# Block 1's first MLP matrix in pairs of tiles, by seven half-width products instead of eight

## The chip, the cores and the metric

The kernel runs on one core of one Trainium2 chip. The metric is the device time of one execution in microseconds; the median of three runs of the kernel before is 1555.03 us (1554.95 to 1555.81). The names used for the engines are those of the profile: PE (TensorE, matmuls), PEld (its weight loads), DVE (VectorE), ACT (ScalarE), POOL (GpSimd) and SP (SyncE, which here only issues DMAs).

## The reference

The whole program is a model of two blocks on 512 tokens of width 1024, in float32. Block 1 is a hybrid mixer (spatial gating and a gated delta rule), cross-attention to a memory of 256 tokens, and a squared-relu MLP; block 2 is a convolution and windowed attention with rotary positions, and a gated MLP. The change concerns block 1's MLP:

```
def squared_relu_mlp(h, w1, w2):
    return jnp.square(jax.nn.relu(h @ w1)) @ w2
...
    x = x + squared_relu_mlp(rmsnorm(x, norm_ffn[l]), ffn_w1[l], ffn_w2[l])
```

Here w1 is 1024 x 4096 and w2 is 4096 x 1024.

## The kernel before

Activations lie feature-major in SBUF: a tile has 128 features on the partitions and 512 tokens in its columns, so x is eight such tiles. A product with a weight matrix is made in output tiles of 128 features; each takes, for every k tile of 128 input features, three matmuls of 512 columns. Float32 precision comes from splitting both operands into a high part (rounded to fp32r) and a low part (the remainder), and from adding high x high, high x low and low x high in PSUM: `mm3`, lines 252 to 254.

The weights arrive in one fixed list (`weight_order`), eight 128x128 tiles to a unit of [128 x 1024]. `prefetch` loads a unit by DMA into one of four buffers `raw` (SP, in written order), ScalarE casts it to `whi` (L217) and VectorE subtracts to get `wlo` (L219); `PF` says that loads run three units ahead and splits one. `defer(n, fn)` puts other work off by n weight tiles of the list. The Tile framework orders the instructions of each engine other than SP; each engine then executes its own list in that order, and waits on semaphores for the other engines.

Block 1's MLP makes its 4096 hidden features, 32 tiles, in four groups of eight. `hidden(n)` makes one tile of h @ w1: 24 matmuls, relu on ScalarE (L1129), a square on VectorE (L1130) and the split into parts (L320 on ScalarE, L321 on VectorE). After eight hidden tiles (and one of the next group, so that TensorE has something to do) come eight tiles of the second matrix, each with k over the group's eight hidden tiles; VectorE multiplies the result by `rb2` (L1145), the row of 1/rms^2 over all tokens, and GpSimd adds it to x (L1147). The norm's row can be multiplied in at the end because the hidden features scale with it; it comes from the sum of squares `acc` of x, which `wide_later` (L402) spreads over all partitions with two matmuls against a matrix of ones (L407 for acc's high part, L408 for its low part), followed by L410 and a reciprocal (L411). It is asked for three weight tiles into the MLP.

Just ahead of the MLP stands the last product of the attention (`xa_wo`): its eight output tiles are added to x (L1090) and split right away, as operands of w1. Behind it the code writes block 2's rotary tables (L1099 to L1120): position times frequency, reduced by multiples of 2 pi, then ScalarE's sine twice (`sinT`, `cosT`). They are small work for VectorE and ScalarE that is carried out beside the first hidden tiles.

Buffers: activations share 74 slots of [128 x 512] (names beginning with t, also `acc`); `whi` and `wlo` have three buffers each.

Of the kernel before, what the change touches and what calls it, by code (L numbers as in the profile page):

```python
# [32 lines left out]
# parts, before a rotation (its halves are swapped by DMA), before block 2's first norm  # L33
# [12 lines left out]
# ---------------------------------------------------------------- weights  # L46
def weight_order():
    """(matrix, k tile, n tile) of the 128x128 weight tiles, as consumed."""
    seq = []

# [26 lines left out]
    for g in range(4):  # L77
        cols("ffn_w1", range(8 * g + (1 if g else 0), 8 * g + 8), r8)
        if g < 3:
            cols("ffn_w1", [8 * g + 8], r8)  # L80
        cols("ffn_w2", r8, range(8 * g, 8 * g + 8))
    # block 2: cb 0-7, cc 8-15, cx 16-23, q 24-27, k 28, v 29, g_conv 30-37, g_attn 38-45
# [14 lines left out]
    return seq  # L97
# [4 lines left out]
# per-partition columns: (name, columns)  # L102
# [13 lines left out]
# constants of the shapes: identity, ones, upper triangle, decay masks, inversion masks  # L116
# [4 lines left out]
def build(tc, A, out, stage=99):  # L121
    nc = tc.nc
    ctx = ExitStack()
    with ctx:
        # loads are issued in the order in which they are written
        ctx.enter_context(tc.manual_schedule(engines={mybir.EngineType.SP}))
        _build(ctx, tc, nc, A, out, stage)


def _build(ctx, tc, nc, A, out, stage):  # L130
# [33 lines left out]
    # ------------------------------------------------------------ loads  # L164
# [24 lines left out]
    # ------------------------------------------------------------ weights  # L189
    order = weight_order()  # L190
# [5 lines left out]
    def prefetch(u, ahead, split_ahead):  # L196
        """half-units of weights from u on: loads, then high and low parts"""
# [7 lines left out]
        for v in range(u, min(u + split_ahead, nu - 1) + 1):  # L205
            if v not in wsp:
# [16 lines left out]

    late = []
# [10 lines left out]
    def nxt(name, k, n, c=1):  # L235
# [4 lines left out]
        if i % 8 == 0:  # L240
            wraw.pop(u - 1, None)
            wsp.pop(u - 1, None)
            prefetch(u, *PF)
        hi, lo = wsp[u]
# [5 lines left out]
    def mm3(ps, ahi, alo, bhi, blo, start, stop):  # L250
        """ps += a.T @ b, a and b given as high and low parts."""
# [4 lines left out]
    def ling(name, n, ks, mv, ps, start=True, stop=True, off=0):  # L256
        """one output tile; a generator, so that other work can go in between"""
# [14 lines left out]
    # ------------------------------------------------------------ interleaving  # L272
    bg = deque()

    def fill(us):
        """the next pieces of background work"""
        t = 0.0
        while bg and t < us:
# [5 lines left out]
            if d is None:      # waits for the chains  # L284
                break
# [82 lines left out]
    def colsum(acc, nt):  # L368
        """token-major column sums over the partitions: [128, nt] in PSUM"""
# [5 lines left out]
    def row_bc(c, nt, dst=None):  # L375
        """[128, nt] columns spread over all partitions as a row of nt*128"""
# [16 lines left out]
    def norm_later(acc, eps, r, at):  # L393
        """r = rstd columns of the squares' sum acc, emitted a few weight tiles later"""
# [7 lines left out]
    def wide_later(acc, eps, rbt, at, square):  # L402
        """rbt = the row of rstd (or its square) over all partitions, a few weight tiles later"""
# [43 lines left out]
    def conv4(ps, j, lst):  # L447
        """causal convolution of 4 taps and silu of projection tile j"""
# [36 lines left out]
    # w_ab: 8 columns of logits, feature-major  # L485
# [13 lines left out]
    def decay():  # L499
        """beta and the decays from their logits"""  # L500
# [19 lines left out]
        # softplus(a) = max(a, 0) + log1p(exp(-|a|)), log1p(e) = 2 atanh(e / (2 + e))  # L520
# [31 lines left out]
        # running and total decay of each chunk of 128  # L552
# [10 lines left out]
    # ------------------------------------------------ gated delta rule, chunks of 128  # L563
# [44 lines left out]
        # k stays as it is: its norms' squares scale the rows of N, which leaves N's inverse  # L608
        # similar, and the values' rows then carry one norm
# [7 lines left out]
        # the blocks of 16 on the diagonal of N, one to a partition  # L617
# [10 lines left out]
    def inv16():  # L628
        """inverses of I - N in all blocks of 16, transposed"""
# [11 lines left out]
    def qprep():  # L641
        """the part that needs q"""
# [24 lines left out]
    def prep2(c):  # L667
# [6 lines left out]
        # U is the inverse of the diagonal blocks of I - N transposed, doubled in size at each step  # L674
# [19 lines left out]
        # the last two doublings have one block (of 32, then 64) above each diagonal  # L694
# [71 lines left out]
    def out_g(c, ET, vn, state):  # L766
        """chunk c of the delta rule's output: normed, feature-major and gated"""
# [16 lines left out]
        # rmsnorm over dv; q's scale comes in here  # L784
# [66 lines left out]
    # ------------------------------------------------ spatial gating; the delta rule's gate  # L851
# [56 lines left out]
    def mix_g():  # L908
        # lower triangle of the mixing weights, transposed [s, g, t]
# [87 lines left out]
    # w_out  # L997
# [12 lines left out]
    # ============================================================ block 1: cross-attention  # L1010
# [76 lines left out]
    xs2 = []  # L1087
    for n in range(8):
        ps = pss[n] if n < 4 else lin("xa_wo", n, range(8), os_)
        V.tensor_add(x[n], x[n], ps)  # L1090
        xs2.append(split(x[n], col("norm_ffn", n)))
        square_acc(acc, x[n], n == 0, eng=V if n == 7 else G)
    if stage == 2:
# [28 lines left out]
    # ============================================================ block 1: squared relu MLP  # L1122
# [3 lines left out]
    def hidden(n):  # L1126
        ps = lin("ffn_w1", n, range(8), xs)
        r = tmp()
        S.activation(r, ps, AF.Relu)  # L1129
        V.tensor_mul(r, r, r)  # L1130
        return split(r)

    hs = []
# [5 lines left out]
    for g in range(4):  # L1139
# [481 lines left out]
```

## Time and profile before

| | before |
|---|---|
| median of 3 runs | 1555.03 us |
| range of the runs | 1554.95 to 1555.81 us |
| span of the profiled execution, which is the only time shown of it | 1555.8 us |
| PE busy | 1534.2 us, 99% |
| PEld busy | 1263.5 us, 81% |
| DVE busy | 926.7 us, 60% |
| ACT busy | 624.7 us, 40% |
| POOL busy | 135.7 us, 9% |
| the MLP of block 1 | 415.10 to 770.70 us |

Busy time is a share of the whole span, over stages of different kinds; the MLP of block 1 is a little under a quarter of it. A matmul's row begins when it is issued and its end is modelled, so rows of consecutive matmuls overlap, and the step from one start to the next is what a matmul costs in a row of them. A row that ends in square brackets tells how long the engine stood idle ahead of it and what ended this. [...]

### The profile page before, as it was taken

Reading aid. Unit: us, or ns where it says so; the run is one execution under the profiler, and the core shown is the slowest. Engines: PE = TensorE matmul, PEld = TensorE weight load, DVE = VectorE, ACT = ScalarE, POOL = GpSimd, SP = SyncE. Lnnn points to the kernel's source line nnn. Section 1 sums busy time; section 2 is a strip of 40 time slices with the busy share of each in tenths; the row PEclk is TensorE's granted clock in tenths of the full one; section 3 lists DMA queues with packets and bytes.
Section 4 is the critical chain, followed back from the end, with each engine's and each line's share of the span. In section 5 each row is a group of like instructions: output and inputs, shape, how many; then the busy total and the mean of one; then the engine's idle time right before and its main releaser. Section 6 shows DMA issues by size and latency. Waiting matters only on the chain.

```text
span 1555.8 us, 18997 instructions
## 1 busy us (share of the span) xinstructions
PE 1534.2 (99%) x7400; PEld 1263.5 (81%) x7400; DVE 926.7 (60%) x1501; ACT 624.7 (40%) x1043; POOL 135.7 (9%) x162
## 2 busy tenths in 40 slices
PE   8999999999999999999999999999999999999996
PEld 6888798888888888888888888888888888888886
DVE  6887575554665454454588777335546555555557
ACT  6665555443442322324544444333334331332243
POOL 0002120200201011010500000000020002001101
PEclk9999999999999999999999999999999999999998
DMA  7133135221322332222134222223322222322321
GB/s 248 29 105 122 58 125 200 95 68 55 102 95 95 95 95 95 95 95 95 54 99 138 86 77 82 82 95 95 95 95 94 94 86 96 101 94 87 102 74 55
DMA packets 51499, 149.80 MB, mean 96 GB/s; under 512 B 9552, under 2 KB 14032, under 8 KB 51408
## 3 DMA queue, kind: packets, MB, share of 16 engines
q1 hardware_dynamic: 51264, 148.32, 29.5%
q8 instruction: 58, 0.95, 0.2%
q10 hardware_dynamic: 144, 0.26, 0.1%
q14 instruction: 33, 0.27, 0.1%
HBM read 143.97 MB, written 3.28 MB: 95 GB/s over the span
## 4 chain that ended last, share of the span: by engine, by line
PE 97%; DVE 2%; ACT 0%; DMA 0%; issue 0%; SPq 0%; DVEq 0%; ACTq 0%
PE mm L252 30%; PE mm L254 30%; PE mm L253 30%; PE sm L254 1%; PE sm L252 1%; PE sm L253 1%; DVE wlo L219 0%; DMA raw<-wts 0%; PE sm L372 0%; PE sm L710 0%; PE sm L1327 0%; PE sm L1329 0%; PE sm L1328 0%; PE sm L504 0%; PE sm L701 0%; PE sm L580 0%
## 5 line engine op out<-in xcount | busy, mean ns | idle before, releaser
L252 PE MATMUL mm<-t,whi 128*128 128x512 f32 (+1 forms) x1944 | 761.7, 392 | 7.9 <-ACT whi L213 7.4
L253 PE MATMUL mm<-t,whi 128*128 128x512 f32 (+1 forms) x1944 | 758.3, 390 | 0.0
L254 PE MATMUL mm<-t,wlo 128*128 128x512 f32 (+1 forms) x1944 | 758.0, 390 | 0.1
L217 ACT CAST whi<-raw 128x1024 fp32r<-128x1024 f32 x254 | 266.4, 1051 | 594.1 <-PE mm L253 409.8
L219 DVE TENSOR_TENSOR wlo<-raw,whi 128x1024 fp32r<-128x1024 f32 x254 | 354.7, 1396 | 151.8 <-ACT whi L217 147.7
L252 PEld LDWEIGHTS mm<-t,whi 128*128 128x128 f32 x1944 | 365.9, 188 | 87.2 <-ACT whi L213 7.4
L254 PEld LDWEIGHTS mm<-t,wlo 128*128 128x128 f32 x1944 | 365.5, 188 | 83.1 <-DVE wlo L219 1.0
L253 PEld LDWEIGHTS mm<-t,whi 128*128 128x128 f32 x1944 | 365.8, 188 | 79.0
L366 POOL TENSOR_TENSOR acc<-acc,tmp 128x512 f32<-128x512 f32 (+1 forms) x37 | 52.9, 1437 | 499.6 <-ACT tmp L362 243.6
L1145 DVE TENSOR_TENSOR tmp<-mm,acc 128x512 f32<-128x512 f32 x32 | 22.1, 692 | 72.6 <-PE mm L254 72.6
L320 ACT CAST t<-tmp 128x512 fp32r<-128x512 f32 (+1 forms) x70 | 41.6, 596 | 51.0 <-DVE tmp L1130 44.8
L1188 DVE TENSOR_TENSOR tmp<-mm,acc 128x512 f32<-128x512 f32 x46 | 31.7, 689 | 49.0 <-PE mm L254 48.3
L321 DVE TENSOR_TENSOR t<-tmp,t 128x512 fp32r<-128x512 f32 (+1 forms) x70 | 46.0, 657 | 23.3 <-ACT t L320 23.1
L1147 POOL TENSOR_TENSOR res<-res,tmp 128x512 f32<-128x512 f32 x24 | 31.0, 1291 | 245.8 <-DVE tmp L1145 237.2
L1428 DVE TENSOR_TENSOR zp<-mm,acc 128x512 f32<-128x512 f32 x22 | 15.2, 691 | 54.7 <-PE mm L254 54.7
L1444 POOL TENSOR_TENSOR res<-res,tmp 128x512 f32<-128x512 f32 x16 | 20.7, 1293 | 261.5 <-DVE tmp L1443 261.5
L1431 DVE TENSOR_TENSOR tmp<-tmp,mm 128x512 f32<-128x512 f32 x22 | 15.1, 686 | 42.7 <-PE mm L254 41.9
L1443 DVE TENSOR_TENSOR tmp<-mm,acc 128x512 f32<-128x512 f32 x16 | 11.1, 691 | 39.6 <-PE mm L254 39.6
L1339 DVE SCALAR_TENSOR_TENSOR tmp<-zp,colt,tmp 128x512 f32<-128x512 f32 x44 | 32.9, 749 | 2.5 <-ACT tmp L1337 1.7
L1430 ACT ACTIVATE tmp<-tmp,colt 128x512 f32<-128x512 f32 x22 | 15.9, 724 | 41.8 <-DVE tmp L1339 41.8
L456 DVE SCALAR_TENSOR_TENSOR tmp<-zp,colt,tmp 128x512 f32<-128x512 f32 x36 | 26.9, 748 | 5.8 <-ACT tmp L452 5.4
L362 ACT ACTIVATE tmp<-res 128x512 f32<-128x512 f32 (+1 forms) x47 | 26.0, 566 | 10.4 <-DVE res L1505 10.4
(349 smaller groups left out, 1356.3 us busy)
## 6 DMA issues: line engine op xcount, KB each, us to landing
raw<-wts SPq DMA_DIRECT2D x259, 512.0 KB, 3.5
res<-xT SPq DMA_DIRECT2D x16, 256.0 KB, 5.3
yT<-t SPq DMA_DIRECT2D x6, 256.0 KB, 2.3
tmp<-tmp SPq DMA_DIRECT2D x20, 64.0 KB, 2.0
gm<-gm SPq DMA_DIRECT2D x4, 256.0 KB, 4.3
dn<-ch SPq DMA_DIRECT2D x4, 256.0 KB, 2.3
tmp<-memT SPq DMA_DIRECT2D x4, 256.0 KB, 2.6
cst<-const SPq DMA_DIRECT2D x1, 576.0 KB, 6.7
```

The costliest lines, as they stand in the source:

```text
L217: S.copy(hi, r)
L219: defer(LO, lambda r=r, hi=hi, lo=lo: V.tensor_sub(lo, r, hi.bitcast(F32)))
L252: PE.matmul(ps, lhsT=ahi, rhs=bhi, start=start, stop=False)
L253: PE.matmul(ps, lhsT=ahi, rhs=blo, start=False, stop=False)
L254: PE.matmul(ps, lhsT=alo, rhs=bhi, start=False, stop=stop)
L320: S.copy(hi, src)
L321: V.tensor_sub(lo, src, hi.bitcast(F32))
L366: eng.tensor_add(acc[:, :w], acc[:, :w], dst[:, :w])
L456: V.scalar_tensor_tensor(out=c, in0=zp[:, 1 + i:1 + i + T], scalar=col("dn_conv", 4 * j + i), in1=c, op0=ALU.mult, op1=ALU.add)
L1147: G.tensor_add(x[n], x[n], t)
L1188: V.tensor_mul(t, ps, rb)
L1339: V.scalar_tensor_tensor(out=c, in0=zp[:, 2 + i:2 + i + T], scalar=col(wname, 3 * j + i), in1=c, op0=ALU.mult, op1=ALU.add)
```

## The change

The first matrix is multiplied in pairs of output tiles. A pair's weights are a matrix of 256 hidden features by 1024 inputs; the k tiles are taken in four pairs (even and odd), so that weights form 2x2 blocks of 128x128, and the tokens are halved into two lots of 256 columns. A 2x2 product of blocks normally needs eight block products; Strassen's algorithm in Winograd's form needs seven, of sums of blocks. So a pair has seven products of four k steps with three matmuls of 256 columns each (84) where two hidden tiles had 48 matmuls of 512 columns.

The sums are made elsewhere. `seven_steps` makes, per pair, the left sums from the raw weights: `s75` (1024 columns wide), `s64` (two halves of 512), and the parts of a (1024), s75, s64 and b (512): three wide casts and one of 512 on ScalarE, three wide subtractions and one of 512 on VectorE. `rights` makes the sums of token halves once, while `xa_wo` finishes. `pairg` runs the products in the order of `SEVEN`, and four VectorE operations from PSUM combine them into `q`, after a ScalarE copy `c0` of the first product. Relu, square and high parts are now ScalarE's, the low parts VectorE's, both put off by `QD`. `ffn_order` sets the order of the pairs and tiles: four pairs, then for each group a pair, four tiles of w2, a pair, four tiles of w2, and two pairs. `whi` and `wlo` get five buffers, of which a pair takes three; activations have 67 slots.

```diff
-NSLOT = 74
-NRAW, NWS = 4, 3
+NSLOT = 67
+NRAW, NWS = 4, 5
+NSR, NQ = 2, 2
+SPREAD = [6, 2]
+QD = [2, 4]
...
+def ffn_order():
+    for i in range(4):
+        yield 1, i, 0
+    for g in range(4):
+        for n in range(8):
+            if g < 3 and n % 4 == 0:
+                yield 1, 4 * g + 4 + n // 4, g + 1
+            yield 2, n, g
+        if g < 3:
+            yield 1, 4 * g + 6, g + 1
+            yield 1, 4 * g + 7, g + 1
...
+    def sevens(u, later):
+        if u not in sevp:
+            load_raw(u, 1)
+            sevp[u] = seven_steps(u)
+        n = SPREAD[0] if later else len(sevp[u][1])
+        todo = sevp[u][1]
+        for j in range(min(n, len(todo))):
+            if later:
+                defer(SPREAD[1] * j, lambda todo=todo: todo and todo.pop(0)())
+            else:
+                todo.pop(0)()
+    def seven_steps(u):
...
+        def s75():
+            t["s75"] = wd(F32, "sraw", NSR)
+            V.tensor_tensor(t["s75"].rearrange("p (a b) -> p a b", a=2), r3,
+                            r1[:, T:].unsqueeze(1).to_broadcast([P, 2, T]), op=ALU.add)
...
+        return op, [
+            both(s75, hi("a", a)),
+            both(lo("a", a), hi("s75s", c)),
+            both(s6, s4),
+            both(lo("s75s", c), hi("s64s", d)),
+            both(hi("b", b), lo("s64s", d)),
+            both(lo("b", b), end),
+        ]
+    SEVEN = [(1, "B11", 0, 0), (5, "V1", 2, 0), (2, "B21", 1, 0), (7, "V7", 2, 1), (3, "B22", 3, 0),
+             (6, "V6", 1, 1), (4, "T4", 3, 1)]
+    def pairg(name, n1, n2, ops, then, kind="mm"):
...
+        for j, (l, r, b, h) in enumerate(SEVEN):
+            if bs[b] is None:
+                bs[b] = bank(kind)
+            ps = bs[b][:, h * H:(h + 1) * H]
+            whi, wlo = lops[l]
+            for p in range(4):
...
+                mm3(ps, whi[:, ks], wlo[:, ks], *ops[p][r], p == 0, p == 3)
...
+            if j == 1:
+                c0 = t2()[:, :H]
+                S.copy(c0, bs[0][:, :H])
...
+        V.tensor_tensor(q4[:, 0:4:3, :], b3(1), bc(c0), op=ALU.add)
+        V.tensor_tensor(q4[:, 1:3, :], b3(2), bc(q4[:, 3, :]), op=ALU.add)
+        V.tensor_add(q4[:, 3, :], bs[2][:, :H], q4[:, 2, :])
+        V.tensor_tensor(q4[:, 1:3, :], b3(3), q4[:, 1:3, :], op=ALU.add)
+        then(q)
...
-        xs2.append(split(x[n], col("norm_ffn", n)))
+        addr(x[n], col("norm_ffn", n))
...
-    for g in range(4):
-        hs += [hidden(n) for n in range(8 * g + (1 if g else 0), 8 * g + 8)]
-        nx = [hidden(8 * g + 8)] if g < 3 else []
-        for n in range(8):
-            ps = lin("ffn_w2", n, range(8 * g, 8 * g + 8), hs, off=8 * g)
...
+    for what, n, g in ffn_order():
+        if what == 1:
+            hidden(n, "sm" if n % 2 else "mm")
+            continue
+        ps = lin("ffn_w2", n, range(8 * g, 8 * g + 8), hs)
```

The order of the instructions moves as follows. In the rows, t and a number is a slot, mm and sm are PSUM banks, whi and wlo the parts of weights, and a name with _49 in brackets a semaphore that this engine raises (DMAHW is a DMA's).

TensorE before, in the third tile of w1, where the two matmuls of `wide_later` stand (L407 and L408, into sm_4091):

```order
L254 MATMUL mm_4156<-t_820_3962,wlo_4122 128x512
L252 MATMUL mm_4156<-t_827_4001,whi_4121 128x512
L407 MATMUL sm_4091<-t_848_4087,ones_r 128x512
L253 MATMUL mm_4156<-t_828_4002,whi_4121 128x512
L254 MATMUL mm_4156<-t_827_4001,wlo_4122 128x512
L408 MATMUL sm_4091<-t_849_4088,ones_r 128x512
L252 MATMUL mm_4156<-t_834_4040,whi_4121 128x512
L253 MATMUL mm_4156<-t_835_4041,whi_4121 128x512
```

They have matmuls of the tile between them and on both sides. TensorE in the changed kernel, at the end of pair 0 (its last product T4, into mm_4244) and the start of pair 1 (its first product B11, into sm_4295); L608 and L609 are what L407 and L408 were:

```order
L455 MATMUL mm_4244<-t_842_4014,wlo_4033 128x256
L453 MATMUL mm_4244<-t_870_4125,whi_4032 128x256
L454 MATMUL mm_4244<-t_871_4126,whi_4032 128x256
L455 MATMUL mm_4244<-t_870_4125,wlo_4033 128x256
L608 MATMUL sm_4195<-t_890_4191,ones_r 128x512
L609 MATMUL sm_4195<-t_891_4192,ones_r 128x512
L453 MATMUL sm_4295<-t_799_3864,whi_4165 128x256
L454 MATMUL sm_4295<-t_800_3865,whi_4165 128x256
L455 MATMUL sm_4295<-t_799_3864,wlo_4166 128x256
```

Both now stand between the two pairs, one right behind the other. VectorE before, from the angle of the rotary tables to the low part of acc (t_849), the operand of L408:

```order
L219 TENSOR_TENSOR wlo_4160<-raw_4072,whi_4159 128x1024 [waits DMAHW5_49,PE_49,Activation_49]
L1108 TENSOR_SCALAR tmp_4054<-tmp_4054 128x512 [waits DVE_49]
L1113 SCALAR_TENSOR_TENSOR tmp_4051<-tmp_4054,tmp_4051 128x512 [waits DVE_49] x3
L1115 TENSOR_SCALAR tmp_4051<-tmp_4051 128x512 [waits DVE_49]
L1117 SCALAR_TENSOR_TENSOR tmp_4051<-tmp_4051 128x512 [waits Activation_49]
L1120 TENSOR_SCALAR sinT<-sinT,colt 128x512
L1118 TENSOR_SCALAR tmp_4051<-tmp_4051 128x512 [waits DVE_49]
L219 TENSOR_TENSOR wlo_4198<-raw_4119,whi_4197 128x1024 [waits DMAHW6_49,PE_49,Activation_49]
L321 TENSOR_TENSOR t_849_4088<-acc_3860,t_848_4087 128x512 [waits Activation_49]
```

Two low parts of weights stand in this stretch. VectorE in the changed kernel, from a low part of pair 2's weights (wlo_4321) to the low part of acc (t_891), the operand of L609; L1315 to L1322 are the rotary tables:

```order
L301 TENSOR_TENSOR wlo_4321<-sraw_4296,whi_4320 128x1024 [waits PE_49,Activation_49]
L1315 SCALAR_TENSOR_TENSOR tmp_4136<-tmp_4139,tmp_4136 128x512 [waits DVE_49] x2
L288 TENSOR_TENSOR sraw_4427<-raw_4291,raw_4293 128x1024 [waits DMAHW2_49,DMAHW0_49]
L1315 SCALAR_TENSOR_TENSOR tmp_4136<-tmp_4139,tmp_4136 128x512 [waits DVE_49]
L1317 TENSOR_SCALAR tmp_4136<-tmp_4136 128x512 [waits DVE_49]
L1319 SCALAR_TENSOR_TENSOR tmp_4136<-tmp_4136 128x512 [waits Activation_49]
L1322 TENSOR_SCALAR sinT<-sinT,colt 128x512
L1320 TENSOR_SCALAR tmp_4136<-tmp_4136 128x512 [waits DVE_49]
L522 TENSOR_TENSOR t_891_4192<-acc_3860,t_890_4191 128x512 [waits Activation_49]
L611 TENSOR_SCALAR acc_4151<-sm_4195 128x512 [waits PE_49]
```

The low part of acc now has wlo_4321 ahead of it, which waits for PE, and a sum of pair 3's weights (sraw_4427), which waits for a DMA. ScalarE in the changed kernel at the same place, where whi_4222 is for pair 1's weights, whi_4298 and whi_4320 for pair 2's, and t_890 is the high part of acc:

```order
L296 CAST whi_4222<-sraw_4203 128x1024 [waits PE_49]
L296 CAST whi_4298<-raw_4158 128x1024 [waits DMAHW6_49,PE_49]
L296 CAST whi_4320<-sraw_4296 128x1024 [waits PE_49]
L1318 ACT_TABLE_LOAD
L1318 ACTIVATE sinT<-tmp_4136 128x512 [waits DVE_49]
L1321 ACTIVATE cosT<-tmp_4136 128x512 [waits DVE_49]
L521 CAST t_890_4191<-acc_3860 128x512
```

Three casts that wait for buffers of PE's products stand ahead of the two sines and of acc's cast. TensorE in the changed kernel at the end of pair 4 (into mm_4752) and the start of pair 5 (into sm_4962):

```order
L453 MATMUL mm_4752<-t_870_4125,whi_4560 128x256
L454 MATMUL mm_4752<-t_871_4126,whi_4560 128x256
L455 MATMUL mm_4752<-t_870_4125,wlo_4561 128x256
L453 MATMUL sm_4962<-t_799_3864,whi_4882 128x256
L454 MATMUL sm_4962<-t_800_3865,whi_4882 128x256
L455 MATMUL sm_4962<-t_799_3864,wlo_4883 128x256
```

Pair 5 begins right behind pair 4, with weights whi_4882 and wlo_4883 that take over the buffers of whi_4560 and wlo_4561.

## Rows read from the trace of the kernel before

**Rows 1.** The head of the page: busy us (share of the span) xinstructions
```profile
span 1555.8 us, 18997 instructions
...
PE 1534.2 (99%) x7400; PEld 1263.5 (81%) x7400; DVE 926.7 (60%) x1501; ACT 624.7 (40%) x1043; POOL 135.7 (9%) x162
```

**Rows 2.** The view of TensorE's waits: us in total, times, longest
```profile
PE mm L252 <- ACT whi L213: 7.4, 1, 7.4
...
PE sm L1511 <- ACT acc L362: 0.7, 1, 0.7
```

**Rows 3.** Windows, the MLP and block 2's end: us, busy by engine, clock, DMA, GB/s
```profile
415.10:770.70 355.60, 355.60 (x1535) 287.97 (x1534) 188.18 (x190) 119.89 (x155) 46.40 (x36) 1.00 0.29 93
...
1515.00:1540.00 25.00, 25.00 (x210) 24.79 (x209) 20.30 (x53) 11.64 (x28) 4.08 (x2) 1.00 0.13 43
```

**Rows 4.** Groups of the MLP's stretch: busy us, mean ns | idle before, releaser
```profile
L219 DVE TENSOR_TENSOR wlo<-raw,whi 128x1024 fp32r<-128x1024 f32 x63 | 103.5, 1643 | 71.5 <-ACT whi L217 70.6
...
L252 PEld LDWEIGHTS mm<-t,whi 128*128 128x128 f32 x502 | 94.2, 188 | 21.9
...
L217 ACT CAST whi<-raw 128x1024 fp32r<-128x1024 f32 x63 | 66.2, 1050 | 181.9 <-PE mm L253 163.9 <-issue 18.1
...
L1147 POOL TENSOR_TENSOR res<-res,tmp 128x512 f32<-128x512 f32 x24 | 31.0, 1291 | 245.8 <-DVE tmp L1145 237.2 <-ACT whi L217 8.6
...
L321 DVE TENSOR_TENSOR t<-tmp,t 128x512 fp32r<-128x512 f32 x32 | 22.1, 690 | 21.0 <-ACT t L320 21.0
...
L1145 DVE TENSOR_TENSOR tmp<-mm,acc 128x512 f32<-128x512 f32 x31 | 21.4, 692 | 70.3 <-PE mm L254 70.3
```

**Rows 5.** VectorE's timeline: start us, us, operation [idle before <-releaser]
```profile
415.30 0.69 DVE L1090 TENSOR_TENSOR res<-res,mm 128x512 f32<-128x512 f32 x1 [2.77 <-PE mm L254]
...
421.73 1.23 DVE L219 TENSOR_TENSOR wlo<-raw,whi 128x1024 fp32r<-128x1024 f32 x1 [1.72 <-ACT whi L217]
...
422.87 0.42 DVE L1108 TENSOR_SCALAR tmp<-tmp 128x512 f32<-128x512 f32 x1
...
423.32 2.14 DVE L1113 SCALAR_TENSOR_TENSOR tmp<-tmp,tmp 128x512 f32<-128x512 f32 x3
...
426.63 0.69 DVE L1117 SCALAR_TENSOR_TENSOR tmp<-tmp 128x512 f32<-128x512 f32 x1 [0.70 <-ACT sinT L1116]
...
427.24 0.48 DVE L1120 TENSOR_SCALAR sinT<-sinT,colt 128x512 f32<-128x512 f32 x1
...
427.63 0.42 DVE L1118 TENSOR_SCALAR tmp<-tmp 128x512 f32<-128x512 f32 x1
...
429.26 0.69 DVE L321 TENSOR_TENSOR t<-acc,t 128x512 fp32r<-128x512 f32 x1
```

**Rows 6.** One group of 256 columns on VectorE, from the groups by line
```profile
L1504 DVE TENSOR_TENSOR tmp<-mm,acc 128x256 f32<-128x256 f32 x16 | 6.7, 418 | 0.4 <-PE mm L254 0.2
```

**Rows 7.** TensorE's timeline: the kernel's start, L407 and L408, the last matmuls
```profile
8.39 0.63 PE L254 MATMUL mm<-t,wlo 128*128 128x512 f32 x1
...
10.10 0.51 PE L252 MATMUL mm<-t,whi 128*128 128x512 f32 x1
...
430.60 0.40 PE L407 MATMUL sm<-t,ones_r 128*128 128x512 f32 x1
...
431.31 0.39 PE L408 MATMUL sm<-t,ones_r 128*128 128x512 f32 x1
...
1543.89 0.70 PE L1511 MATMUL sm<-acc,cst 128*128 128x256 f32 x2 [0.74 <-ACT acc L362]
```

**Rows 8.** ScalarE's timeline at the rotary tables and the cast of acc
```profile
425.96 0.63 ACT L1116 ACTIVATE sinT<-tmp 128x512 f32<-128x512 f32 x1 [2.97 <-DVE tmp L1115]
...
428.63 0.60 ACT L320 CAST t<-acc 128x512 fp32r<-128x512 f32 x1
```

**Rows 9.** The DMA issues of the page: KB each, us to landing
```profile
raw<-wts SPq DMA_DIRECT2D x259, 512.0 KB, 3.5
```

**Rows 10.** A window behind the last matmul, columns as in rows 3
```profile
1546.50:1547.00 0.50, 0.00 (x0) 0.00 (x0) 0.47 (x2) 0.00 (x0) 0.00 (x0) 0.50 0.00 0
```

More of the change, by code (lines that the diff above doesn't have):

```diff
@@ L49, in weight_order, with pair @@
     seq = []
+    seven = set()
+    def pair(name, n1, n2):
+        assert len(seq) % 8 == 0
+        seven.add(len(seq) // 8)
+        for n, o in ((n1, 0), (n2, 1), (n1, 1), (n2, 0)):
+            for k in range(o, 8, 2):
+                seq.append((name, k, n))
     def cols(name, ns, ks):
@@ L76, in weight_order @@
     cols("xa_wo", range(4, 8), r8)
-    for g in range(4):
[L78 to L81, printed above, removed]
+    for what, i, g in ffn_order():
+        if what == 1:
+            pair("ffn_w1", 2 * i, 2 * i + 1)
+        else:
+            cols("ffn_w2", [i], range(8 * g, 8 * g + 8))
     cols("w_in_2", [28, 29, 24, 25, 26, 27], r8)
@@ L187, in _build @@
     ones_r = cp.tile([P, P], F32R, name="ones_r")
-    order = weight_order()
+    order, seven = weight_order()
     wst = {"i": 0}
@@ L205, in prefetch @@
         for v in range(u, min(u + split_ahead, nu - 1) + 1):
-            if v not in wsp:
+            if v in seven:
+                sevens(v, v > u)
+            elif v not in wsp and v - 1 not in seven:
                 r = wraw[v]
@@ L222, in prefetch, with load_raw @@
                 wsp[v] = (hi, lo)
+    def load_raw(u, ahead):
+        for v in range(u, min(u + ahead, nu - 1) + 1):
+            if v not in wraw:
+                r = wp.tile([P, 1024], F32, tag="raw", bufs=NRAW, name=nm("raw"))
+                nc.sync.dma_start(out=r, in_=A["wts"][v])
+                wraw[v] = r
+    sevp = {}
+    def sevens(u, later):
[7 more added lines that the diff above has]
+                defer(SPREAD[1] * j, lambda todo=todo: todo and todo.pop(0)())
+            else:
+                todo.pop(0)()
@@ new lines, in seven_steps, with hi, f, lo @@
+    def seven_steps(u):
+        r0, r1 = wraw[u], wraw[u + 1]
+        wd = lambda dt, tag, b: wp.tile([P, 1024], dt, tag=tag, bufs=b, name=nm(tag))
+        r3 = r0.rearrange("p (a b) -> p a b", a=2)
+        op = {}
+        t = {}
+        def s75():
+            t["s75"] = wd(F32, "sraw", NSR)
+            V.tensor_tensor(t["s75"].rearrange("p (a b) -> p a b", a=2), r3,
+                            r1[:, T:].unsqueeze(1).to_broadcast([P, 2, T]), op=ALU.add)
+        def hi(n, src):
+            def f():
+                s = src()
+                w = s.shape[-1]
+                t[n] = (wd(F32R, "whi", NWS), wd(F32R, "wlo", NWS)) if w > T else (t2(F32R), t2(F32R))
+                S.copy(t[n][0], s)
+            return f
+        def lo(n, src):
+            def f():
+                V.tensor_sub(t[n][1], src(), t[n][0].bitcast(F32))
+            return f
+        def s6():
+            t["s64"] = wd(F32, "sraw", NSR)
+            V.tensor_add(t["s64"][:, :T], t["s75"][:, T:], r0[:, :T])
+        def s4():
+            V.tensor_add(t["s64"][:, T:], t["s64"][:, :T], r1[:, :T])
+        def both(*fs):
+            def f():
+                for g in fs:
+                    g()
+            return f
+        def end():
+            h = lambda n, j: tuple(a[:, j * T:(j + 1) * T] for a in t[n])
+            op.update({1: h("a", 0), 4: h("a", 1), 7: h("s75s", 0), 5: h("s75s", 1),
+                       6: h("s64s", 0), 3: h("s64s", 1), 2: t["b"]})
+        a, b = (lambda: r0), (lambda: r1[:, :T])
+        c, d = (lambda: t["s75"]), (lambda: t["s64"])
+        return op, [
[6 more added lines that the diff above has]
+        ]
@@ L243, in nxt @@
             prefetch(u, *PF)
+            if u + 2 in seven and u + 1 not in seven:
+                sevens(u + 2, True)
         hi, lo = wsp[u]
@@ L1124, in _build, with hidden, then, relu @@
     wide_later(acc, 1e-6, rb2, 3, True)
[L1126 to L1133, printed above, removed]
+    def hidden(i, kind):
+        def then(q):
+            hs[2 * i] = [t2(F32R), t2(F32R)]
+            hs[2 * i + 1] = [t2(F32R), t2(F32R)]
+            def relu():
+                for j in range(2):
+                    S.activation(q[:, j * T:(j + 1) * T], q[:, j * T:(j + 1) * T], AF.Relu, scale=1.0 - 2 * j)
+                S.activation(q, q, AF.Square)
+                for j in range(2):
+                    S.copy(hs[2 * i + j][0], q[:, j * T:(j + 1) * T])
+            def low():
+                for j in range(2):
+                    hi, lo = hs[2 * i + j]
+                    V.tensor_sub(lo, q[:, j * T:(j + 1) * T], hi.bitcast(F32))
+            defer(QD[0], relu)
+            defer(QD[1], low)
+        for _ in pairg("ffn_w1", 2 * i, 2 * i + 1, xs, then, kind):
+            pass
+    hs = {}
     acc = acc_tile()
@@ L1546, in layout @@
     W["w_attn_out_2"] = W["w_attn_out_2"][hp]
-    order = weight_order()
+    order, _ = weight_order()
     assert len(order) % 8 == 0
```

94 lines of the change are left out of this document (80 added, 14 removed).

## The prediction

> **What bounds the kernel now.** I read the page's head first: TensorE's matmuls stand at 99% of a span of 1555.8 us, VectorE at 60%, ScalarE at 40% [rows 1]. Then the view of TensorE's waits: one of 7.4 us at the very start, and then nothing over 0.7 [rows 2]. So whatever shortens TensorE's stream shortens the time, and whatever makes TensorE wait lengthens it, since today it waits nowhere in the stretch that the change touches. Third, a table of windows: the MLP of block 1 runs from 415.10 to 770.70 with 1535 matmuls in 355.60 us at a granted clock of 1.00, 0.2317 us from one matmul of 512 columns to the next; VectorE is busy for 188 of these 356 us. The second row of that table is the end of block 2, where the kernel already runs matmuls of 256 columns: 210 in 25.00 us, 0.119 us each [rows 3].
>
> **The products.** Two tiles of the first matrix cost 2 x 8 x 3 = 48 matmuls of 512 columns, 48 x 0.2317 = 11.12 us. A pair by seven products costs 7 x 4 x 3 = 84 matmuls of 256 columns, 84 x 0.119 = 10.00 us. Sixteen pairs save 16 x 1.12 = 18.0 us. This row is the same operation at the same size, so I take it. At exactly half of 0.2317 it would be 22.3, and at 0.120 16.7; these are the ends.
>
> The matmul row is a modelled one, so the loads deserve a look of their own. A load takes 188 ns [rows 4], more than the 119 ns from one 256-column matmul to the next, and 84 loads replace 48; but 209 loads began in those 25.00 us, so they overlap one another. [...]
>
> **The work around the products** is a different matter: sums of weights, their high and low parts, and four combinations from PSUM. Per pair VectorE gets four operations of 1024 columns (1.23 us alone [rows 5]), three of 512, three combinations of 512 and two low parts (0.69 each [rows 4]), and one combination of 256 (0.42 [rows 6]): 4.92 + 8 x 0.69 + 0.42 = 10.86 us against 10.00 of TensorE. The forms that add one half to both halves of a wide tile are not in the trace; I take them at the rows of their size, which may be off by a third of a microsecond each either way. A tile of the second matrix costs VectorE 0.69 + 1.23, or about 2.9 where its subtraction stretches beside a GpSimd add (the mean over the stretch is 1.64 [rows 4]), of 24 x 0.2317 = 5.56 us. A group of four pairs and eight tiles then has 4 x 10.86 + 8 x 2.9 = 67 us on VectorE against 40.0 + 44.5 = 84.5 on TensorE, so in the later groups it hides. ScalarE has some 7.6 us per pair (four of 1024 at 1.05 and six smaller ones), and hides too.
>
> **Where it does not hide: the end of the first pair.** The two matmuls that spread the sum of squares (L407 and L408; L608 and L609 now) stand in the middle of the third tile today, 15.5 us after the stage's start, and L408 begins 1.36 us after its operand is done at 429.95: it waited for nothing [rows 5, 7]. Now both stand behind the 84th matmul of the first pair and ahead of the second pair's first. TensorE runs in order, so all of pair 1 waits for L609's operand. That operand is VectorE's subtraction of `acc`, and on its queues stand, ahead of it, the rotary tables with their two sines, and the preparation of pairs 1 and 2, whose five buffers come free only as pair 0 ends.
>
> I walk that queue. Call the end of pair 0 T. ScalarE's cast `whi_4222` needs a buffer that pair 0's V7 product frees 15 matmuls before the end, at T - 1.8, and takes 1.05, so VectorE takes up `wlo_4223` at T - 0.75. From there VectorE runs without a gap up to the sine: three low parts and one sum of 1024 columns (4.6 us at the 1.14 us from which one follows another [rows 5]; `wlo_4321` itself needs a buffer that the last product frees, which is met by then), two adds of 512 (1.2), the conversion, scaling and rounding of the angle (four at 0.45, 1.8), and the three reductions and the limit (2.14 + 0.45 [rows 5]). That is 10.2, so T + 9.45. Then the alternation that the trace shows as it is: sine 0.63, VectorE's 0.69, 0.48 and 0.42 for the next angle, cosine 0.63 likewise, cast 0.60, subtraction 0.69 [rows 5, 8]; before, this took 4.0 us, from the sine's start at 425.96 to the subtraction's end at 429.95. So the subtraction ends near T + 13.4; since rows overlap a little at each hand-over on one engine, I put the wait at **13.2 us**. The table load for the sines hides under VectorE's part. The sum of 1024 columns for pair 3 also needs a DMA, which is issued once a sum ahead has read the old block, some 4.1 us earlier; a block lands in 3.5 [rows 9], so it is just met, and 1 us late at worst. Ends of this term: 12 if wide operations follow each other faster than their rows, 15.5 with the DMA late and the queue behind when it gets there.
>
> In such a gap the clock falls. At the end of the kernel the granted clock stands at 0.50 from 1546.5, after TensorE's last matmul at 1544.6 [rows 7, 10], and at the kernel's start, where TensorE begins at 7.4 [rows 2], the four matmuls from 8.39 to 10.10 take 0.43 us each where 0.23 would do [rows 7]. From 7.4 to 10.10 some six run at that pace; 6 x 0.2, and the step back, are about **1.3 us** for a restart. [...] Without the restart the sum would be 1.3 less.
>
> **The smaller waits**, each at a place where the new order puts a matmul right behind work that needs its predecessor's end. Pair 0 needs all eight updates of x, and the last is written at 415.30 to 415.99 [rows 5]; its high and low parts and sums are one chain over ScalarE and VectorE to the last operand: 0.9. Pairs 2 and 3, 0.65 together. Pair 4's B21 waits for a cast queued behind one that needs the product just ended (1.05 + 0.6 and hand-overs): 2.0. Pair 5's first product stands right behind pair 4's last, and its weights' buffer is the one that this last product frees: a cast of 1.05 and a low part whose start of 1.23 is partly covered by two matmuls: 2.4. Two later w2 tiles wait for the copy c0 queued likewise, 0.7 each; the last pair's end 0.5. That is 7.9; I give it 3 to 12.
>
> **The sum** against the profile's own span: -18.0 + 13.2 + 1.3 + 7.9 = +4.4 us. The span of 1555.8 equals the slowest of the three runs shown (1555.81) and is 0.8 above their median, so I set the sum on the median: 1555.0 + 4.4 = **1559.4 us**. With the ends: -22.3 + 12 + 0 + 3 = -7, and -16.7 + 15.5 + 1.3 + 12 = +12.
>
> **Rivals.**
> 1. The wait at pair 0 stands, but the smaller waits are covered by slack I don't see, as the order gives only distances. Then -18.0 + 14.5 = -3.5, 1551.5 us. For it: between these places TensorE has runs of 48 matmuls and more that wait for nothing. Against: at pair 5 the producer of the awaited buffer is the matmul just ahead.
> 2. The wait is not there, because VectorE gets to `acc` in time; the gain comes through less the small waits: -18 + 3 or so, 1540 us. For it: VectorE is at 60% [rows 1]. Against: a first-in first-out queue with pair 0's last matmul on it can't be early.
> 3. VectorE becomes the bound of the later groups, and the change is slower still. The wide subtraction takes twice its 1.23 us beside a GpSimd add; if all four wide operations of a pair did, a pair would be at 10.86 + 4 x 1.03 = 15.0, and a group at 83 of 84.5 us. Where the group's third and fourth pair follow one another, VectorE would fall 2 x 5 us behind with some 6 of lead: about 4 per group, 12 in three: 1571 us. It decides from about 15 us a pair. Against: only 24 adds, of 1.29 us each [rows 4], fall in the stretch.
> 4. The loads bind: 84 x 0.188 = 15.8 us a pair, 4.7 more than now, +75 and the waits: some 1650 us. Against: the overlap seen above.
>
> **Chances.** Forecast 0.57, with a range of its own of 1556 to 1565; rival 1 0.17, rival 2 0.08, rival 3 0.16, rival 4 0.02. About 0.2%, 3.1 us, is what a measurement can tell here. Below 1551.9 lie rival 2 and half of rival 1: faster 0.17. The other half and the low fifth or so of the forecast lie within: same 0.22. The rest is slower, 0.61. The range for all, 1549 to 1568, leaves out rival 2 and the far parts of 3 and 4.
>
> **What would show it.** In the profile after, TensorE's waits should have one line of 12 to 15 us, for L609 on VectorE's low part of `acc`, between about 426 and 440, with the granted clock below 1.00 in it. Pairs clear of waits should last 10.0 us; pair 5's first product should wait some 2 us. Block 2 and everything up to 390 us should be as before. A pair far from 10.0, no wait at 426, or waits repeated in all groups would each prove one of the steps wrong.

## The result, and the profile after

| | before | after |
|---|---|---|
| median | 1554.99 us (4 runs, 1554.77 to 1555.81) | 1568.17 us (4 runs, 1567.29 to 1569.03) |
| ratio to before | | 1.0083, 95% interval 1.0069 to 1.0097 |
| span of the profiled execution | 1555.8 us | 1565.4 us |

The changed kernel is 13.2 us slower. The forecast was slower, by 4.4 us, at 1559.4; the measured median lies 0.2 us above the upper end of the range for all and 3.2 above the forecast's own range (1556 to 1565). The direction and the main mechanism held, and the size did not.

The two spans differ by only 9.6 us, because before's profiled execution lost some 2.4 us to a clock dip in the mixer (its later runs have spans of about 1553.4 us for times of 1555.2, and some 1.8 us lie around a span); traces are therefore compared stage by stage here. The prediction took the span of 1555.8 for the time of the slowest run; it set its sum on the median, so nothing followed from that. Before's row for that dip, from its table of windows (us, busy by engine, granted clock, DMA share, GB/s):

```profile
160.00:170.00 10.00, 10.00 (x63) 8.02 (x57) 2.01 (x7) 3.06 (x11) 0.00 (x0) 0.66 0.14 50
```

The head of the page after, and its chain of waits, answer to [rows 1]. TensorE is busy for less time and is still what ends last, but VectorE, ScalarE and other engines now stand in that chain for a tenth of it. The chain before:

```profile
PE 97%; DVE 2%; ACT 0%; DMA 0%; issue 0%; SPq 0%; DVEq 0%; ACTq 0%
```

After:

```profile
span 1565.4 us, 20466 instructions
...
PE 1522.1 (97%) x7976; PEld 1282.8 (82%) x7976; DVE 1015.6 (65%) x1637; ACT 677.0 (43%) x1123; POOL 144.5 (9%) x162
...
PE 90%; DVE 6%; ACT 2%; issue 1%; DMA 1%; POOL 0%; SPq 0%; DVEq 0%; ACTq 0%; POOLq 0%
```

TensorE's waits in the MLP, which answer to [rows 2], where there were none: us in total, times, longest.

```profile
PE sm L608 <- ACT t L521: 12.2, 1, 12.2
PE mm L453 <- ACT t L521: 2.2, 1, 2.2
PE mm L453 <- ACT t L296: 2.0, 2, 1.8
PE sm L453 <- ACT whi L296: 1.6, 1, 1.6
PE sm L455 <- DVE wlo L301: 1.6, 1, 1.6
PE mm L453 <- ACT t L371: 1.2, 2, 0.6
PE mm L454 <- DVE t L522: 0.8, 1, 0.8
```

The first is the wait at the end of pair 0. The rest are pair 0's own operands (2.2, 0.8 and 0.2 of the 2.0), pair 4's B21 (1.8), pair 5's start (1.6 and 1.6) and two w2 tiles behind c0 (1.2). TensorE's timeline around the first wait:

```profile
427.44 0.28 PE L455 MATMUL mm<-t,wlo 128*128 128x256 f32 x1
439.93 0.80 PE L608 MATMUL sm<-t,ones_r 128*128 128x512 f32 x1 [12.21 <-ACT t L521]
440.66 0.80 PE L609 MATMUL sm<-t,ones_r 128*128 128x512 f32 x1
441.25 0.41 PE L453 MATMUL sm<-t,whi 128*128 128x256 f32 x1
...
445.52 0.34 PE L455 MATMUL sm<-t,wlo 128*128 128x256 f32 x1
```

Pair 0 ends at T = 427.72. From 441.25 to 445.52 twenty matmuls of 256 columns take 0.21 us each where 0.118 is usual. VectorE's timeline beside it, as the prediction walked it from T - 0.75:

```profile
426.96 1.22 DVE L301 TENSOR_TENSOR wlo<-sraw,whi 128x1024 fp32r<-128x1024 f32 x1 [2.94 <-ACT whi L296]
...
432.98 1.41 DVE L1315 SCALAR_TENSOR_TENSOR tmp<-tmp,tmp 128x512 f32<-128x512 f32 x2
434.31 1.22 DVE L288 TENSOR_TENSOR sraw<-raw,raw 128x1024 f32<-128x1024 f32 x1
...
437.28 0.69 DVE L1319 SCALAR_TENSOR_TENSOR tmp<-tmp 128x512 f32<-128x512 f32 x1 [0.69 <-ACT sinT L1318]
...
439.91 0.69 DVE L522 TENSOR_TENSOR t<-acc,t 128x512 fp32r<-128x512 f32 x1 [1.20 <-ACT t L521]
```

It starts at T - 0.76, never idles until the sine, and ends with the low part of acc at 440.60. The granted clock of TensorE (last but two of the columns, a share of full speed) answers to [rows 3], where it is 1.00 all through:

```profile
418.50:421.50 3.00, 2.88 (x13) 2.89 (x14) 3.00 (x6) 0.23 (x1) 0.00 (x0) 0.50 0.44 157
432.00:440.00 8.00, 0.07 (x1) 0.07 (x1) 6.03 (x10) 1.89 (x4) 0.00 (x0) 0.50 0.16 58
441.00:445.00 4.00, 4.00 (x19) 3.90 (x19) 3.51 (x3) 0.00 (x0) 0.00 (x0) 0.50 0.00 0
490.00:493.00 3.00, 3.00 (x11) 2.55 (x10) 2.90 (x6) 0.00 (x0) 0.00 (x0) 0.50 0.83 287
```

Three times TensorE works at a granted clock of 0.50, called half speed here (0.21 us a step for 256 columns and 0.43 for 512, against 0.118 and 0.2317): behind pair 0's waits, behind the long one, and behind pair 5's. A pair that waits for nothing, here pair 9, begins at the first of these rows and ends ahead of the last, 84 matmuls in 9.90 us:

```profile
598.26 0.28 PE L453 MATMUL sm<-t,whi 128*128 128x256 f32 x1
...
608.04 0.28 PE L455 MATMUL sm<-t,wlo 128*128 128x256 f32 x1
608.16 0.39 PE L453 MATMUL mm<-t,whi 128*128 128x512 f32 x1
```

**The account.** From pair 0's first matmul (412.22) to the first of the next norm (784.11) the stage takes 371.9 us; before, 415.10 to 775.86, 360.8. Laid out over all steps from one matmul's start to the next, at 0.2317 us for 512 columns and 0.118 for 256: the products save 768 x 0.2317 - 1344 x 0.118 = 19.3 us. Steps that end in a wait add 23.1, steps at half speed 5.5, and steps a little longer than these two values 2.3. Together +11.6. The difference of the two stages is 11.1, because before has one matmul of block 2 more in its stage (0.2) and steps that add up to 0.2 above these values. From there to its last two matmuls block 2 takes 769.3 us instead of 768.0, with that one matmul now in it. The whole is 11.1 + 1.3 = +12.4. The profiled execution of the change took 1567.29 us, the fastest of the four, 12.3 above before's median; that the medians differ by 13.2 is the 0.9 by which it lies below its own.

### The profile page after: what moved, and what is told of

Same layout as the page of the kernel before. It is cut to its first block, busy times and chain, and to the rows that moved or that the text cites. A ratio compares the mean times of both kernels' runs of the same rounds, so it can differ in the third digit from the quotient of the medians.

```text
span 1565.4 us, 20466 instructions
## 1 busy us (share of the span) xinstructions
PE 1522.1 (97%) x7976; PEld 1282.8 (82%) x7976; DVE 1015.6 (65%) x1637; ACT 677.0 (43%) x1123; POOL 144.5 (9%) x162
## 4 chain that ended last, share of the span: by engine, by line
PE 90%; DVE 6%; ACT 2%; issue 1%; DMA 1%; POOL 0%; SPq 0%; DVEq 0%; ACTq 0%; POOLq 0%
PE mm L453 26%; PE mm L455 26%; PE mm L454 26%; PE sm L455 3%; PE sm L453 2%; PE sm L454 2%; DVE wlo L301 1%; DVE t L522 1%; DVE wlo L251 1%; DMA raw<-wts 1%; ACT whi L249 0%; ACT t L1082 0%; PE sm L573 0%; DVE t L1742 0%; ACT whi L296 0%
## 5 line engine op out<-in xcount | busy, mean ns | idle before, releaser
L453 PE MATMUL mm<-t,whi 128*128 128x512 f32 (+1 forms) x1880 | 716.0, 381 | 10.4 <-ACT whi L245 6.5
L454 PE MATMUL mm<-t,whi 128*128 128x512 f32 (+1 forms) x1880 | 712.6, 379 | 0.8 <-DVE t L522 0.8
L455 PE MATMUL mm<-t,wlo 128*128 128x512 f32 (+1 forms) x1880 | 712.3, 379 | 0.1
L249 ACT CAST whi<-raw 128x1024 fp32r<-128x1024 f32 x222 | 232.2, 1050 | 429.7 <-PE mm L454 288.9
L251 DVE TENSOR_TENSOR wlo<-raw,whi 128x1024 fp32r<-128x1024 f32 x215 | 283.3, 1318 | 79.1 <-ACT whi L249 76.2
L301 DVE TENSOR_TENSOR wlo<-sraw,whi 128x1024 fp32r<-128x1024 f32 x32 | 46.2, 1443 | 28.5 <-ACT whi L296 28.2
L453 PE MATMUL sm<-t,whi 128*128 128x256 f32 (+1 forms) x200 | 58.3, 292 | 1.6 <-ACT whi L296 1.6
L455 PE MATMUL sm<-t,wlo 128*128 128x256 f32 (+1 forms) x200 | 58.1, 291 | 1.6 <-DVE wlo L301 1.6
L454 PE MATMUL sm<-t,whi 128*128 128x256 f32 (+1 forms) x200 | 58.1, 291 | 0.0
L296 ACT CAST whi<-sraw 128x1024 fp32r<-128x1024 f32 x32 | 33.5, 1047 | 56.0 <-PE mm L454 42.2
L453 PEld LDWEIGHTS sm<-t,whi 128*128 128x128 f32 x200 | 38.9, 195 | 2.3 <-ACT whi L296 1.8
L455 PEld LDWEIGHTS sm<-t,wlo 128*128 128x128 f32 x200 | 38.8, 194 | 2.2 <-DVE wlo L301 1.8
```

The lines of the kernel that those rows point to most:

```text
L249: S.copy(hi, r)
L251: defer(LO, lambda r=r, hi=hi, lo=lo: V.tensor_sub(lo, r, hi.bitcast(F32)))
L296: S.copy(t[n][0], s)
L301: V.tensor_sub(t[n][1], src(), t[n][0].bitcast(F32))
L453: PE.matmul(ps, lhsT=ahi, rhs=bhi, start=start, stop=False)
L454: PE.matmul(ps, lhsT=ahi, rhs=blo, start=False, stop=False)
```

## The experiments

Each is an edit of the changed kernel unless the text says otherwise; the verdict is against the kernel before on the same chip (medians 1555.3 to 1555.7).

**Only the two spreading matmuls moved.**

```diff
-    wide_later(acc, 1e-6, rb2, 3, True)
+    wide_later(acc, 1e-6, rb2, 36, True)
```

> The two matmuls that spread the sum of squares are asked for 36 weight tiles into the MLP instead of 3; all else stands. Theory (the loss is their place in TensorE's order, behind pair 0 and ahead of pair 1): the 12.2 us wait at pair 0's end and its half-speed stretch (2.8 us) go, a smaller wait of up to 4 us may appear at their new place at the start of pair 3, 1553 to 1558 us. Rival (VectorE has too much to do there, rotary tables and two pairs' weights, and some matmul must wait whatever the order): pair 1 or 2 waits instead, and the time falls by less than 5 us, 1563 or more.

Measured: 1568.69 us, ratio 1.0085 (1.0071 to 1.0098), no gain at all. Two of TensorE's waits in the MLP, and ScalarE's timeline at the larger one:

```profile
PE mm L453 <- ACT t L371: 12.1, 4, 9.6
...
PE sm L608 <- ACT t L521: 1.4, 1, 1.4
```

```profile
439.38 0.63 ACT L1318 ACTIVATE sinT<-tmp 128x512 f32<-128x512 f32 x1 [4.09 <-DVE tmp L1317]
441.50 0.63 ACT L1321 ACTIVATE cosT<-tmp 128x512 f32<-128x512 f32 x1 [1.49 <-DVE tmp L1320]
442.04 0.35 ACT L371 COPY t<-mm 128x256 f32<-128x256 f32 x1
```

The spreading matmuls now wait 1.4 us at their new place, and ahead of that pair 2 waits 9.6 us for the copy c0 (L371), which stands on ScalarE behind the two sines. So my theory of their place in TensorE's order falls, and what the rival said comes to pass, another pair waits: whoever comes behind the sines waits. The sines wait for VectorE's angle, and that for low parts of weights whose buffers pair 0 frees.

**Only the rotary tables moved,** as a function with the lines from `posi` to the last product with the sign, behind six tiles of the second matrix.

```diff
+        if (what, n, g) == (2, 6, 0):
+            rotary()
```

> The rotary tables are written behind six tiles of the second matrix instead of ahead of the MLP; the two spreading matmuls are asked for as before. In the order they now stand inside pair 0's last two products, and the subtraction of acc ahead of all low parts that wait for pair 0. Theory: the 12.2 us wait and its half-speed stretch vanish, 1552 to 1554 us. Rival (VectorE too busy): the rotary tables leave, so it gains too, but the wide low parts still hold pair 1 for some 5 us: 1558 or more.

Measured: 1554.98 us, ratio 0.9995 (0.9986 to 1.0003): 13.2 us faster than the change, no different from before, and 1.0 above the expected range. No wait is over 2.2 us now:

```profile
PE mm L453 <- ACT t L371: 2.6, 3, 1.2
PE mm L453 <- ACT t L521: 2.2, 1, 2.2
PE sm L455 <- DVE wlo L301: 2.0, 1, 2.0
PE sm L453 <- ACT whi L296: 1.9, 1, 1.9
PE mm L454 <- DVE t L522: 0.8, 1, 0.8
```

The same account for its stage: -19.3, waits +13.0, half speed +4.3, longer steps +1.0. The rotary tables at this place are worth all of the measured loss, and what is left of waits and clock still eats the products' gain. What the run does not separate is the tables' own work from the weights' that stands with them: in the changed kernel VectorE spends some 3.9 us on the tables and 5.8 on the preparation of weights between 426.96 and the first sine at 436.62, and the edit takes the first away and puts acc's low part ahead of the second (L609, which reads it, runs at 428.38 there, ahead of pair 0's end at 429.83).

**Both edits.**

> Both edits at once. Theory: nothing is left to gain over the move of the rotary tables alone, 1552 to 1554 us, within 1 us of that run. Rival (VectorE too busy): the two add up, each with a part, and this run is at least 3 us below either.

Measured: 1555.45 us, ratio 1.0000 (0.9991 to 1.0009), 0.5 above the run with the tables alone moved and inside its spread: nothing adds up, as the theory had it; 1.5 above its range.

**The long wait filled.**

```diff
+FILL = 102
...
+        for _ in range(FILL):
+            PE.matmul(ps[:, :256], lhsT=ones_r, rhs=xs[3]["T4"][0], start=True, stop=True)
+        PE.matmul(ps, lhsT=ones_r, rhs=hi, start=True, stop=False)
...
```

> The wait stays as long, but TensorE works in it: 102 matmuls of 256 columns (12.1 us at 0.118), whose result is overwritten, fill it, and the two spreading matmuls come after the first products of pair 1. Theory (of the loss at this place some 3 us are the half-speed stretch behind the wait, 26 matmuls at 0.21 instead of 0.118 and two of 512 at 0.7): pair 1 starts at the same moment and runs at full clock, 1564.5 to 1565.5 us. Rival (the clock costs nothing beside the wait, because VectorE's work in those 5.6 us would hold TensorE anyway): 1567.5 to 1568.5.

Measured: 1566.91 us, ratio 1.0072 (1.0060 to 1.0085), 1.3 below the change and between the two; the intervals of the two ratios overlap. The fillers run from 429.07, and pair 1 starts at 441.04, at full clock:

```profile
429.07 12.13 PE L1334 MATMUL sm<-t,ones_r 128*128 128x256 f32 x102
441.04 0.28 PE L454 MATMUL sm<-t,whi 128*128 128x256 f32 x1
```

```profile
440.00:450.00 10.00, 10.00 (x83) 9.73 (x82) 8.79 (x12) 3.39 (x6) 0.00 (x0) 1.00 0.16 54
```

Pair 0 starts at 413.66 here and at 412.22 in the change, so pair 1 follows 27.4 us behind it instead of 29.0, of which 1.3 are the two spreading matmuls that no longer stand between. Steps at half speed fall from 5.5 to 3.1 us; c0's waits rise from 1.2 to 2.5 and pair 5's from 3.2 to 3.9, and pair 4's fall from 1.8 to 0.5. From pair 0's first matmul to the norm's first this execution takes 369.0 us instead of 371.9: 2.8 less, about what the theory gave. Against the change's profiled execution it loses 1.4 of them ahead of the stage and 1.0 behind it, in code that the edit leaves as it is. So the stage speaks for the theory, and the medians of the whole kernel do not decide.

**TensorE's order fixed by hand,** with the rotary tables moved: no first product of pair 5 behind pair 4, and pair 0's first k steps ahead.

```diff
+        if n1 == 0:
+            four = (0, 1, 4, 2)
+            steps = [(j, p) for j in four for p in range(3)] + [(j, 3) for j in four] + \
+                [(j, p) for j in (3, 5, 6) for p in range(4)]
...
-    wide_later(acc, 1e-6, rb2, 3, True)
+    wide_later(acc, 1e-6, rb2, 18, True)
...
+    with tc.manual_schedule(engines={mybir.EngineType.PE}):
...
```

> On top of the move of the rotary tables: TensorE's order in the MLP is fixed as written, so pair 5 no longer begins right behind pair 4; pair 0 runs the k steps that don't need x's last two tiles first, for its first four products; the two spreading matmuls stand just behind the start of pair 1. Theory (the small waits are places in TensorE's order, each with its half-speed stretch): pair 0's 3.1 us of waits and 1.7 us of half speed shrink to some 2, pair 5's 3.9 and 1.0 vanish, 1547 to 1551 us. Rival (VectorE has more work than time while pairs follow one another, 10.9 us against 10.0, so what is taken from one wait appears in the next): 1553 or more.

Measured: 1556.68 us, ratio 1.0003 (0.9995 to 1.0012). The theory falls: pair 5 no longer waits, but w2's first tile now waits 2.1 us for c0, and pair 0 waits 1.7 and 1.5 us for other operands. The waits add up to 14.6 us (13.0 before this edit), half speed to 5.3. The longest of the waits:

```profile
PE mm L458 <- ACT t L1344: 2.4, 1, 2.4
```

It stands at 731 us, where the run before this edit has none: in the order as written, the first w2 tile behind the last pair waits for that pair's own hidden features. With the short wait next to it, it makes 3.1 of the 14.6. That is the order and not VectorE's load, so the run does not show the rival's reason; how much of the rest is VectorE's is not shown by it.

**The kernel before with the new buffer counts** (67 slots, five pairs of weight buffers).

> The kernel before with the changed kernel's buffer counts (67 slots, five pairs of weight buffers) and nothing else. After the MLP the changed kernel takes 1.3 us longer than before over the same matmuls of block 2, with steps of 0.2325 us instead of 0.2317 in its first half. If that comes from where the buffers lie, this kernel is 1 us slower than before, 1556 to 1556.5 us; if it comes from the order of block 2's other work or from the execution, it is within 0.4 us of before.

Measured: 1556.19 us, ratio 1.0002 (0.9993 to 1.0011). The time lies in the range named for the buffers, but before stands at 1555.66 on this chip, and the interval takes in both branches, so the time does not decide. From the norm's first matmul to the last two it takes 768.0 us, as before does with one matmul less, so the trace gives no sign that block 2's longer time comes from there.

**Both longer waits filled,** with the rotary tables moved.

```diff
+FILL = {0: 24, 10: 32}
...
+        if n1 in FILL:
+            bs[0] = bank(kind)
+            for _ in range(FILL[n1]):
+                PE.matmul(bs[0][:, :H], lhsT=ones_r, rhs=ops[0]["B11"][0], start=True, stop=True)
```

> The kernel with the rotary tables moved, and in its two longest waits TensorE works: 24 matmuls of 256 columns ahead of pair 0's first product, 5 and 27 around the end of pair 4, all overwritten by the products that follow. They take 2.8 and 3.8 us, about as long as the waits of 3.1 and 3.9 that they stand in. Theory (each of these waits also costs a stretch at half speed behind it, 1.7 and 1.0 us or more): 1552 to 1553.5 us. Rival (ScalarE and VectorE are what pairs wait for; with TensorE faster behind the wait, the time comes back as waits further on): 1554.5 to 1555.5.

Measured: 1553.10 us, ratio 0.9981 (0.9973 to 0.9990): faster than the kernel before by 0.2% and than the change by 1.0%, and 1.9 below the run without fillers. The windows behind pair 0's and pair 5's waits in it:

```profile
420.00:430.00 10.00, 9.72 (x69) 9.34 (x69) 8.32 (x13) 5.57 (x9) 0.00 (x0) 0.84 0.15 52
...
470.00:480.00 10.00, 10.00 (x69) 9.20 (x68) 8.28 (x11) 6.18 (x11) 0.00 (x0) 1.00 0.33 116
```

Without fillers the two windows have a granted clock of 0.76 and 0.83. Waits (7.4 us) and fillers (56 x 0.118 = 6.6) make 14.0, 1.0 more than the waits had been; half speed falls from 4.3 to 1.3. Work that nobody needs, put where TensorE would idle, gained the difference here: 2.0 us by this account, 1.9 in the median.

**One wide operation less for VectorE,** with the rotary tables moved.

```diff
-            both(hi("b", b), lo("s64s", d)),
+            hi("b", b),
...
```

> The kernel with the rotary tables moved, and without the low part of s64, one subtraction of 1024 columns per pair on VectorE; the products that need it take the high part twice, so two of a pair's seven products are not the reference's. TensorE and ScalarE do the same work as before. Theory (VectorE's 10.9 us per pair against 10.0 on TensorE set the pace of the first pairs, which is why a wait that is taken away returns elsewhere): its waits of 13 us fall by 4 or more, 1549 to 1551.5 us. Rival (the waits are on single casts and buffers at fixed places): less than 1.5 us, 1553.5 or more.

Measured: 1552.47 us, ratio 0.9973 (0.9962 to 0.9983), 2.5 below. The waits fall from 13.0 to 9.6 us, and half speed rises from 4.3 to 5.1. The stage is 1.8 us shorter. Pair 0's waits shrink by 1.2, while pair 5's stay:

```profile
PE sm L456 <- ACT whi L296: 2.0, 1, 2.0
PE sm L458 <- DVE wlo L301: 1.8, 1, 1.8
PE mm L456 <- ACT t L524: 1.5, 1, 1.5
```

Between the two theories: VectorE's load is part of pair 0's waits, and pair 5's are a matter of one cast and one buffer.

## Why the prediction was right in direction and short in size

- **The products** were put at -18.0 and gave -19.3, since the step is 0.118 and not 0.119 us. In the pair shown above 84 loads of 188 ns, 15.8 us in sum, took 9.9 us with the products, so they overlap and did not bind: rival 4 is out.
- **The wait at pair 0** was put at 13.2 and measured 12.2, with the queue as it was walked: the walk's start is right to 0.01 us against the pair's end, and its end, the low part of acc, came 12.9 behind T, not 13.4. The table load for the sines, 1.28 us from 428.83, lay under VectorE's work, which went on until the sine at 436.62. The wait stands at L608, for acc's cast, and not at L609 as the prediction named it: L609 begins at 440.66, right behind the low part's end at 440.60. So L608's step is 0.73 us where 0.43 is a step of 512 columns at half speed (six of them stand at 490.9 to 493.4), and some 0.3 us that the account has under the clock are the end of this wait. That it is VectorE's and ScalarE's queue, and not TensorE's order, is what the prediction left half said and what the first two experiments show: move the matmuls and the time stays; move the tables and 13.2 us are back.
- **The clock** is the term that failed most: 1.3 us for one restart against 5.5 for three. The restart behind the long wait alone covers 20 matmuls at 0.21 and two of 512 columns at 0.6 to 0.7, some 2.7 us; the start of the kernel [rows 7] was too short a model of it, and there the step of 0.43 us alone speaks for the clock, as the window from 7.40 to 10.10 us shows it as 1.00. And two groups of waits that I priced as bare waits, each of 3.2 us in pieces, cost another 1.2 and 1.5 us. The fillers show that this is a cost of its own: with both groups filled, 3.0 us less of half speed, 1.9 less time; with the long wait filled, 2.4 less of half speed and a stage 2.8 shorter.
- **The smaller waits** were put at 7.9, and without the long one the steps with a wait add 10.7, of which 9.5 are idle. Pair 4 (1.8 against 2.0) and c0 (1.2 against 1.4) were right; pair 5 is 3.2 against 2.4; pair 0 is 3.2 against 0.9, because VectorE was already behind when it began (it is busy for 3.00 of the 3.00 us from 418.5, in the row above), and I walked only the last tile's own chain. The 0.65 put for pairs 2 and 3 is there, but in pieces too short for the list of waits: seven single steps at 458 and at 467 to 469 us are longer by 0.7 in all.
- **Longer steps** were not in the sum: 2.3 us in the stage and, without the one matmul more, 1.1 in block 2, where steps are 0.2325 instead of 0.2317 us in the first 200 us. Of the 2.3, 1.7 are single steps: the seven just named, and the first behind eight of the waits, which goes with the wait. What lengthens block 2 stays open. The buffer counts give no sign of it, and it does not come with every variant: from the norm to the last two matmuls the other traces of the changed kernel have 769.1 to 770.4 us, and the one with TensorE's order fixed has 767.5.
- **Rivals.** The wait stood, so rival 2 is out, and the smaller waits were not covered, so rival 1 is. Rival 3's 1571 us lies nearer to the measured time than the forecast's 1559.4, but that is luck, as it named the wrong place: two of the later groups lose 0.6 us each, in one wait behind c0. The longer subtraction that it builds on is in the trace of before: a wide subtraction took 2.29 us at 500.10, beside a GpSimd add of 1.29 from 500.02, and 1.22 at 516.81 with no add beside it. VectorE is short of time at the start, where pairs follow one another and the sums of tokens are still being made; that its load there is part of the waits is what the run with one wide operation less shows (13.0 to 9.6 us).

By the account the profiled execution misses the forecast's +4.4 by 8.0 us: +4.2 of clock, +3.1 of longer steps (those that before has too taken off), +2.0 of waits and -1.3 of products. The median misses it by 8.8, since that execution was the fastest of the four. So the mechanism held, the wait at pair 0 was sized to 1 us, and the step that failed is the price of the clock: one restart of 1.3 us, where each of three groups of waits has its own stretch at half speed.

## What to carry to other kernels

Fewer matmuls on the engine that bounds a kernel are only worth what the engines that prepare their operands can keep up with (here the products saved 19.3 us and steps that end in a wait added 23.1): ask what stands ahead of each operand on its in-order queue at the moment when buffers come free, and look there for unrelated work, such as these rotary tables. Price each wait of the bounding engine together with the half-speed work behind it, also where the wait is only a few microseconds in pieces (here two groups of waits of 3.2 us each had 1.2 and 1.5 us of it). When an order is changed to remove a wait, look for the next reader of the same queue before counting the gain (here c0, which held TensorE for 9.6 us in the first experiment).

## What the runs showed of the hardware

TensorE's clock fell not only in the wait of 12.2 us (0.50 in the windows from 432 to 445 us) but also around waits of 2.2, 0.2 and 0.8 us close together (0.50 from 418.5 to 421.5), and behind two of 1.6 with two matmuls between them: at 490 to 493 us TensorE is fully busy, and the granted clock is 0.50. So two groups of short waits in this kernel had a stretch at half speed too, and filling such waits with overwritten matmuls, with the rotary tables moved, took the clock of the window from 470 to 480 us from 0.83 to 1.00 (pair 5) and that of the window from 420 to 430 us from 0.76 to 0.84 (pair 0).

The length of a short wait alone did not tell whether this happens. Pair 4 waits 1.81 us in the change and in the run with only the spreading matmuls moved. Behind it the granted clock is 1.00 in the first and 0.50 in the second, with TensorE busy in both. What differs ahead of it is that the second had waited 1.4 us at 461.7, 1.3 at 468.0 and 0.2 at 470.1; that this is the reason is not shown. The windows of the two:

```profile
480.00:486.00 6.00, 5.75 (x48) 5.55 (x47) 4.73 (x8) 2.64 (x4) 0.00 (x0) 1.00 0.58 200
```

```profile
481.00:484.00 3.00, 3.00 (x17) 3.00 (x16) 2.85 (x5) 0.01 (x1) 0.00 (x0) 0.50 0.69 233
```
